# Latent attention's matmuls pinned to the order in which the program names them, and memory weights split one piece ahead

## Chip, cores and metric

The kernel runs on one core of a Trainium2 chip. The metric is the device time of one execution in microseconds (us). A core has five engines that run side by side, each with an instruction queue of its own: TensorE (PE: matmuls and transposes; its weight loads are listed as PEld), VectorE (DVE), ScalarE (ACT), GpSimd (POOL) and SyncE (SP, which issues DMAs). They wait for each other through semaphores.

## What is computed

One decoder layer on 1024 tokens of width 1024, in float32. Two head groups read one input projection: gated linear attention, and latent attention (8 heads, keys of 96, values of 64). Their outputs are joined and projected; then come cross-attention to 256 memory tokens and a gated feed-forward with a short convolution. The part that the change touches, with the memory keys and values:

```python
q = to_heads(rms_norm(c_q, mla_q_a_norm[l]) @ mla_w_uq[l], MLA_HEADS)
kv = to_heads(rms_norm(c_kv, mla_kv_a_norm[l]) @ mla_w_ukv[l], MLA_HEADS)
k_nope, v = kv[..., :MLA_NOPE], kv[..., MLA_NOPE:]
...
q = rms_norm(q, mla_q_norm[l])
k = rms_norm(k, mla_k_norm[l])
...
o_mla = from_heads(causal_block_attention(q, k, v))   # blocks of 128 queries
...
mn = rms_norm(mem, norm_mem[l])
xkv = (mn @ xa_w_kv[l]).reshape(b, mem.shape[1], 2, XA_HEADS, XA_HEAD_DIM)
xk = rms_norm(xkv[:, :, 0], xa_k_norm[l])
xv = xkv[:, :, 1]
```

## The kernel before

Products with weights, and the scores, use **rounded** operands: a float32 array is split into a high and a low part (`split`: one pass on ScalarE, then one on VectorE), and `mm3` sums three matmuls. Transposes and the value products of latent attention use **exact** float32 operands.

The latent attention runs as a loop over slots j. Slot j belongs to one of 64 heads: two groups of four heads, and for each group eight query blocks of 128 tokens (a unit u), so a unit takes four slots. For each head these steps are needed:

- `att_s` (S): scores of one or two blocks of keys, with the mask added by one further matmul; VectorE takes the maximum and ScalarE the exponential, into `p`. It stands two slots ahead of the head that it is for.
- `att_t` (PTp): transposes of `p`, four at most to a PSUM bank. There is one bank; a pass of ScalarE or VectorE moves it to `pT`.
- `att_o` (mo): value products of two heads at a time. Each writes 64 columns of the array, and the two heads alternate between its halves.
- `prep_c`, `prep_kv`, `prep_q`, `prep_kt`, `prep_qt`: what a later unit needs; `kTp` and `qTp` are the transposes of its keys and queries, which `split` turns into KTh, KTl and QT. `att_r` (rr) transposes the reciprocal row sums once in a unit.

`mem_kv` is a generator. It projects the memory tokens to keys and values (`mo_kv`, 16 pieces of a weight of 256 rows by 256 columns), normalises the keys (`mks`) and transposes them (`mkt`). `filler` takes steps of it at the end of each slot. While it still has steps, `pr_` uses one PSUM bank for kv, q, kTp, qTp and rr. The split weights `mwh` and `mwl` have one buffer each.

What the engines run is not the written order: a scheduler lays the instructions of each engine out ahead of time, by priority (the written order) and by when it reckons them ready. `tc.keep_in_program_order(i)` ties an instruction behind the one that was written just before it on its engine. `o_gla` (otp) transposes the other group's output in the last eight slots.

Of the kernel before, what the change touches and what calls it, by code (L numbers as in the profile page):

```python
# [10 lines left out]
F32 = mybir.dt.float32  # L11
# [4 lines left out]
ALU = mybir.AluOpType  # L16
# [17 lines left out]
def build(tc, a, out):  # L34
# [25 lines left out]
    def k16(shape, dt, name):  # L60
        return big.tile(shape, dt, name=name, tag="k16", bufs=8)

    mm = nc.tensor.matmul

    def act(o, i, f, **kw):
        nc.scalar.activation(out=o, in_=i, func=f, **kw)  # L66

    def tt(o, x, y, op, eng=None):
        (eng or nc.vector).tensor_tensor(out=o, in0=x, in1=y, op=op)  # L69
# [7 lines left out]
    def split(hi, lo, src, gain=None):  # L77
        if gain is None:
            act(hi, src, AF.Copy)
            tt(lo, src, f32(hi), ALU.subtract)  # L80
        else:
            act(hi, src, AF.Copy, scale=gain)
            stt(lo, src, gain, f32(hi), ALU.mult, ALU.subtract)
# [55 lines left out]
    def col(r):  # L139
        return cols[:, r:r + 1]  # L140
# [9 lines left out]
    def small(shape, name, bufs=3):  # L150
        return smp.tile(shape, F32, name=name, tag=name, bufs=bufs)
# [4 lines left out]
    def rsqrt(dst, ssq, n, inv, post=None, nm="ra"):  # L156
        yy = small([P, 8], nm + "_y", 2)[:, 0:n]
        act(yy, ssq, AF.Ln, scale=inv, bias=epsc)
        act(yy, yy, AF.Exp, scale=-0.5)
        ms = small([P, 8], nm + "_m", 2)[:, 0:n]  # L160
        nc.vector.tensor_scalar(out=ms, in0=ssq, scalar1=inv, scalar2=EPS, op0=ALU.mult, op1=ALU.add)
        tq = small([P, 8], nm + "_t", 2)[:, 0:n]
        tt(tq, yy, yy, ALU.mult)
        stt(tq, tq, -0.5, ms, ALU.mult, ALU.mult)
        stt(yy if post else dst, tq, 1.5, yy, ALU.add, ALU.mult)
        if post is not None:
            nc.vector.tensor_scalar(out=dst, in0=yy, scalar1=post, scalar2=None, op0=ALU.mult)
# [415 lines left out]
    def pr_(shape, name):  # L583
        prn[0] += 1
        pl = prn[1] if prn[1] is not None else (prc, pjc[2])[prn[0] % 2]
        return sub(pl, shape, name)
# [91 lines left out]
    def prep_kt(u):  # L678
        G = grps[u.gi]
        tok = slice(u.t * P, (u.t + 1) * P)  # L680
        kp = pr_([MQK, 4, P], "kTp")
        for h in range(4):
            nc.tensor.transpose(kp[:, h], u.kn[:, h], ident)
        split(G[1][:, :, tok], G[2][:, :, tok], kp, cols[0:MQK, R_MK:R_MK + 1])

    def prep_qt(u):
        qp = pr_([MQK, 4, P], "qTp")
        for h in range(4):
            nc.tensor.transpose(qp[:, h], u.qn[:, h], ident)
        qt = qtc.tile([P, 2, 4, P], F32R, name="QT", tag="qt", bufs=3)  # L690
        u.QTh, u.QTl = qt[0:MQK, 0], qt[0:MQK, 1]
        split(u.QTh, u.QTl, qp, cols[0:MQK, R_MQ:R_MQ + 1])
# [30 lines left out]
    def att_t(x, b):  # L723
        k0, k1 = 4 * b, min(x.u.t + 1, 4 * b + 4)
        tp = pjc[0].tile([P, 4, P], F32, name="PTp", tag="pj", bufs=1)
        for k in range(k0, k1):
            nc.tensor.transpose(tp[:, k - k0], x.p[:, k * P:(k + 1) * P], ident)  # L727
        x.pT[b] = m.tile([P, 4, P], F32, name="pT", tag="pT", bufs=4)
        evac[0] += 1
        if evac[0] % 5 == 0:  # L730
            nc.vector.tensor_copy(out=x.pT[b][:, 0:k1 - k0], in_=tp[:, 0:k1 - k0])
        else:
            act(x.pT[b][:, 0:k1 - k0], tp[:, 0:k1 - k0], AF.Copy)

    def att_r(u):

        ri = m.tile([P, 4, MV], F32, name="ri", tag="ri", bufs=2)
        r4 = small([P, 4], "xri", 2)
        nc.vector.reciprocal(out=r4, in_=u.rs)
        nc.gpsimd.tensor_copy(out=ri, in_=r4.unsqueeze(2).broadcast_to([P, 4, MV]))  # L740
        rp = pr_([P, 2, P], "rr")
        for i in range(2):
            nc.tensor.transpose(rp[:, i], ri[:, 2 * i:2 * i + 2].rearrange("p h v -> p (h v)"), ident)
        u.r = m.tile([P, 2, P], F32, name="rT", tag="ri", bufs=2)
        act(u.r, rp, AF.Copy)

# [33 lines left out]
    def mem_t(i):  # L780
        if i == 0:
            MN.append(k16([P, 2, KD, MEM], F32R, "mn"))
        bs = slice((i // 2) * P, (i // 2 + 1) * P)
        tp = pr_([P, 4, P], "mtp")
        k0 = 4 * (i % 2)
        for k in range(4):
            nc.tensor.transpose(tp[:, k], MB[i // 2][:, (k0 + k) * P:(k0 + k + 1) * P], ident)
        split(MN[0][:, 0, k0:k0 + 4, bs], MN[0][:, 1, k0:k0 + 4, bs], tp)

    def mem_kv():  # L790
        mn = MN[0]
        for n in range(4):
            o = pr_([P, 2, 256], "mo_kv")
            for hk in range(4):
                raw = mk.tile([P, 2, 256], F32, name="mraw", tag="raw", bufs=2)
                nc.sync.dma_start(out=raw, in_=a["xa_w_kv"][hk * 256:(hk + 1) * 256, n * 256:(n + 1) * 256]
                                  .rearrange("(k p) n -> p k n", p=P))
                hi = mk.tile([P, 2, 256], F32R, name="mwh", tag="wh", bufs=1)
                lo = mk.tile([P, 2, 256], F32R, name="mwl", tag="wl", bufs=1)
                for j in range(2):  # L800
                    split(hi[:, j], lo[:, j], raw[:, j], col(R_NE + 2 * hk + j))
                yield
                for b in range(2):
                    bs = slice(b * P, (b + 1) * P)
                    for i in range(2):
                        lh, ll = mn[:, 0, 2 * hk + i, bs], mn[:, 1, 2 * hk + i, bs]
                        mm(o[:, b], lhsT=ll, rhs=hi[:, i], start=hk == 0 and b == 0 and i == 0, stop=False)
                        mm(o[:, b], lhsT=lh, rhs=lo[:, i], start=False, stop=False)
                        mm(o[:, b], lhsT=lh, rhs=hi[:, i], start=False, stop=hk == 3 and b == 1 and i == 1)
                yield  # L810
            if n >= 2:
                act(xv[:, :, (n - 2) * 256:(n - 1) * 256], o, AF.Copy)
                continue
            ks = mk.tile([P, 4, P], F32, name="mks", tag="raw", bufs=2)
            kq = mk.tile([P, 4, P], F32, name="mkq", tag="wl", bufs=1)
            ss = small([P, 4], "xss", 2)
            act(ks, o.rearrange("p b (h d) -> p (b h) d", h=2), AF.Copy)
            act(kq, ks, AF.Square)
            nc.vector.tensor_reduce(out=ss, in_=kq, axis=AX.X, op=ALU.add)
            r = small([P, 4], "xr", 2)  # L820
            rsqrt(r, ss, 4, 1.0 / XD)
            tt(ks, ks, r.unsqueeze(2).broadcast_to([P, 4, P]), ALU.mult)
            yield
            tp = pr_([P, 2, 2, P], "mkt")
            for b in range(2):
                for h in range(2):
                    nc.tensor.transpose(tp[:, h, b], ks[:, 2 * b + h], ident)
            split(xk[:, 0, 2 * n:2 * n + 2], xk[:, 1, 2 * n:2 * n + 2], tp.rearrange("p h b i -> p h (b i)"), col(R_XK))

    fill = [mem_kv()]  # L830

# [46 lines left out]
    def o_gla(t):  # L878
        if not oh:
            o_pair(0)  # L880
        tok = slice(t * P, (t + 1) * P)
        tp = pr_([P, 4, P], "otp")
        for k in range(4):
            nc.tensor.transpose(tp[:, k], og[:, t, k * P:(k + 1) * P], ident)
        split(oh[0][:, :, tok], ol[0][:, :, tok], tp)

    def wo_pc(i, n):
# [13 lines left out]
    for j in range(-2, NS + 1):  # L901
        if j == JT:
            filler(1000)
            mkp.__exit__(None, None, None)
            mpp.__exit__(None, None, None)
            pw = pool("pw", "right"); pwc = pw.__enter__()
            with pri(-1000):
                W = [wo_pc(i, 0) for i in range(3)]
        if NS - NB <= j < NS:
            o_gla(j - NS + NB)  # L910
        A = hs_[j] if 0 <= j < NS else None
        B = hs_[j - 1] if j >= 1 else None
        C = hs_[j + 2] if j + 2 < NS else None
        if A:
            att_t(A, 0)
        if B and B.h % 2:
            att_o(hs_[j - 2], B, B.nh - 1)
        if C:
            att_s(C, 0)
        prep_slot(j)  # L920
        if A and A.h == 3:
            att_r(A.u)
        if A and A.nh == 2:
            att_t(A, 1)
            if A.h % 2:
                att_o(B, A, 0)
        if C and C.nh == 2:
            att_s(C, 1)
        if j >= 0:
            filler(2)  # L930
    mps.__exit__(None, None, None)
    prs.__exit__(None, None, None)
    for p_ in pjp[::-1]:
# [679 lines left out]
```

## Time and profile before

| | us |
|---|---|
| median of 3 runs (1373.0 to 1375.1) | 1374.26 |
| the profiled execution | 1373.4 |
| its span, first to last instruction | 1371.7 |
| TensorE busy, whole span | 1332.3 |
| VectorE busy, whole span | 929.2 |
| ScalarE busy, whole span | 648.1 |

TensorE is busy for 97% of the span. The slots of latent attention lie between 257 and 486 us. Busy time is the time in which some instruction of an engine is recorded as running; ends of matmuls are modelled, so where two matmuls stand behind each other it is the distance of their starts that tells what one costs.

### The profile page before, as it was taken

The page shows a single profiled execution, that of the slowest core. Times are in us where ns is not written, and L with a number is a line of the kernel's source. Part 1 is how long each engine was busy: PE and PEld are TensorE (multiplying, and loading weights), DVE is VectorE, ACT ScalarE, POOL GpSimd, SP SyncE. Part 2 cuts the span into 40 slices and gives each one's busy share as a digit, 9 for nine tenths or more (in the row PEclk, how much of TensorE's full clock was granted, in tenths as well). Part 3 has the DMA queues.
Part 4 walks back from the last instruction along what each step waited for, and adds up shares of the span by engine and source line. Part 5 has one row for each costly group of instructions (what it writes and reads, how often), then busy time and mean ns, then how long its engine had stood idle before and what let it go on. Part 6 is the DMA issues. An engine that isn't in the chain of part 4 may idle for free.

```text
span 1371.7 us, 19161 instructions
## 1 busy us (share of the span) xinstructions
PE 1332.3 (97%) x7240; PEld 1111.0 (81%) x7240; DVE 929.2 (68%) x1712; ACT 648.1 (47%) x1316; POOL 204.1 (15%) x318
## 2 busy tenths in 40 slices
PE   8999999999999999999997989999999999999998
PEld 8977789878777787888875767888888888888887
DVE  6545785786687635377778887677766777678562
ACT  6424447776776713275544434344333335334440
POOL 0210001322232000000021433322333220000000
PEclk9999999999999999999998999999999999999999
DMA  7121010111002213110121332223332226963331
GB/s 216 39 63 31 1 47 20 40 54 43 9 1 77 72 68 106 48 37 39 65 92 62 116 115 77 96 90 115 116 115 104 97 85 229 330 223 134 120 130 62
DMA packets 80621, 122.93 MB, mean 90 GB/s; under 512 B 7305, under 2 KB 48400, under 8 KB 80528
## 3 DMA queue, kind: packets, MB, share of 16 engines
q1 hardware_dynamic: 80354, 121.64, 26.4%
q8 instruction: 57, 0.93, 0.3%
q14 instruction: 36, 0.29, 0.1%
q10 hardware_dynamic: 174, 0.06, 0.0%
HBM read 93.11 MB, written 28.57 MB: 89 GB/s over the span
## 4 chain that ended last, share of the span: by engine, by line
PE 85%; DVE 7%; issue 3%; ACT 3%; DMA 1%; POOL 1%; SPq 0%; DVEq 0%; ACTq 0%; POOLq 0%
PE pj L88 6%; PE pj L89 6%; PE pj L90 6%; PE P L1220 6%; PE P L1222 6%; PE P L1221 6%; PE dn L1558 5%; PE dn L1557 5%; PE dn L1556 5%; PE mo L756 3%; PE PTp L727 2%; PE A L1221 2%; PE A L1222 2%; PE A L1220 2%; PE S L88 2%
## 5 line engine op out<-in xcount | busy, mean ns | idle before, releaser
L1220 PE MATMUL P<-obP,op 128*128 128x512 f32 x352 | 139.3, 396 | 8.2 <-DVE GU L69 8.1
L1222 PE MATMUL P<-obP,op 128*128 128x512 f32 x352 | 138.2, 393 | 0.0
L1221 PE MATMUL P<-obP,op 128*128 128x512 f32 x352 | 138.2, 393 | 0.0
L1556 PE MATMUL dn<-wk 128*128 128x512 f32 x308 | 119.9, 389 | 0.0
L1557 PE MATMUL dn<-wk 128*128 128x512 f32 x308 | 119.8, 389 | 0.0
L1558 PE MATMUL dn<-wk 128*128 128x512 f32 x308 | 119.8, 389 | 0.0
L66 ACT ACTIVATE op<-ss 128x512 fp32r<-128x512 f32 x88 | 55.0, 629 | 121.4 <-PE P L1222 78.1
L69 POOL TENSOR_TENSOR ss<-rw 128x512 f32<-128x512 f32 x42 | 55.2, 1336 | 279.1 <-DVE op L69 248.2
L69 DVE TENSOR_TENSOR op<-rw,op 128x512 fp32r<-128x512 f32 x58 | 63.2, 1089 | 40.0 <-ACT op L66 40.0
L1220 PEld LDWEIGHTS P<-obP,op 128*128 128x128 f32 x352 | 66.9, 190 | 25.2 <-DVE GU L69 11.3
L1222 PEld LDWEIGHTS P<-obP,op 128*128 128x128 f32 x352 | 66.8, 190 | 14.1
L1221 PEld LDWEIGHTS P<-obP,op 128*128 128x128 f32 x352 | 67.0, 190 | 13.8
L66 ACT ACTIVATE op<-rw 128x512 fp32r<-128x512 f32 x58 | 36.6, 631 | 79.5 <-PE P L1222 59.3
L1556 PEld LDWEIGHTS dn<-wk 128*128 128x128 f32 x308 | 57.8, 188 | 12.4 <-DVE hq L69 0.2
L1557 PEld LDWEIGHTS dn<-wk 128*128 128x128 f32 x308 | 57.8, 188 | 12.0
L1558 PEld LDWEIGHTS dn<-wk 128*128 128x128 f32 x308 | 57.8, 188 | 12.0
L66 ACT ACTIVATE wk<-wq 128x1024 fp32r<-128x1024 f32 x28 | 29.7, 1061 | 74.6 <-PE dn L1558 56.3
L69 DVE TENSOR_TENSOR op<-ss,op 128x512 fp32r<-128x512 f32 x88 | 63.2, 726 | 1.1 <-ACT op L66 0.4
L72 DVE SCALAR_TENSOR_TENSOR conv<-GU,cols,conv 128x1023 f32<-128x1023 f32 (+1 forms) x44 | 57.1, 1297 | 3.7 <-ACT conv L66 3.3
L717 DVE TENSOR_REDUCE mx<-S 128x1 f32<-128x128 f32 (+7 forms) x64 | 48.0, 752 | 15.5 <-PE S L715 15.2
L1221 PE MATMUL A<-fl,op 128*128 128x512 f32 x144 | 56.0, 389 | 0.0
L1222 PE MATMUL A<-fh,op 128*128 128x512 f32 x144 | 56.0, 389 | 0.0
(434 smaller groups left out, 3740.7 us busy)
## 6 DMA issues: line engine op xcount, KB each, us to landing
ga<-gP SPq DMA_DIRECT2D x35, 512.0 KB
rw<-in_ffn_w_gate SPq DMA_DIRECT2D x11, 1024.0 KB
rw<-in_ffn_w_up SPq DMA_DIRECT2D x11, 1024.0 KB
gP<-GU SPq DMA_DIRECT2D x44, 256.0 KB
gP<-conv SPq DMA_DIRECT2D x33, 256.0 KB
wq<-in_ffn_w_down SPq DMA_DIRECT2D x16, 512.0 KB
mraw<-in_xa_w_kv SPq DMA_DIRECT2D x16, 256.0 KB
hh<-in_x SPq DMA_DIRECT2D x2, 2048.0 KB
```

Source lines behind the costliest of these rows:

```text
L66: nc.scalar.activation(out=o, in_=i, func=f, **kw)
L69: (eng or nc.vector).tensor_tensor(out=o, in0=x, in1=y, op=op)
L72: nc.vector.scalar_tensor_tensor(out=o, in0=x, scalar=s, in1=y, op0=op0, op1=op1)
L88: mm(o, lhsT=ll, rhs=rh, start=i == 0, stop=False)
L89: mm(o, lhsT=lh, rhs=rl, start=False, stop=False)
L90: mm(o, lhsT=lh, rhs=rh, start=False, stop=last and i == n - 1)
L1220: mm(o, lhsT=wl, rhs=bh[:, k], start=start and k == 0, stop=False, **kw)
L1221: mm(o, lhsT=wh, rhs=bl[:, k], start=False, stop=False, **kw)
L1222: mm(o, lhsT=wh, rhs=bh[:, k], start=False, stop=k == 3, **kw)
L1556: mm(bk[t], lhsT=gl, rhs=wh, start=first and g == 0 and k == 0, stop=False, **kw)
L1557: mm(bk[t], lhsT=gh, rhs=wl, start=False, stop=False, **kw)
L1558: mm(bk[t], lhsT=gh, rhs=wh, start=False, stop=end, **kw)
```

## The change

Inside the slots (from j = 0 on) every matmul and transpose that goes through `mm` and `transpose` is pinned behind the one written before it. The slot is written in another order: the transposes for keys, queries and row sums come behind `att_t` and `att_o`, then the scores and the other preparations, then one step of `mem_kv` (from j = -1 on; it was two steps from j = 0 on), and only then the second score block, `att_t` and `att_o`. In short slots (`late`) the second score block comes last. In `mem_kv` the weight of piece x+1 is loaded and split right behind the matmuls of piece x, and the transposes `mkt` come one step behind the matmuls whose sums they need.

```diff
-    mm = nc.tensor.matmul
+    PIN = [False]
+    def pinned(i):
+        if PIN[0]:
+            tc.keep_in_program_order(i)
+        return i
+    def mm(*args, **kw):
+        return pinned(nc.tensor.matmul(*args, **kw))
+    def transpose(*args):
+        return pinned(nc.tensor.transpose(*args))
...
     def mem_kv():
-        for n in range(4):
-            o = pr_([P, 2, 256], "mo_kv")
-            for hk in range(4):
-                raw = mk.tile([P, 2, 256], F32, name="mraw", tag="raw", bufs=2)
...
-                yield
...
+        pieces = [(n, hk) for n in range(4) for hk in range(4)]
+        w = weights(0, 0)
+        yield
+        for x, (n, hk) in enumerate(pieces):
...
+            if hk == 3 and n < 2:
+                ks = mk.tile([P, 4, P], F32, name="mks", tag="raw", bufs=2)
...
+                act(ks, o.rearrange("p b (h d) -> p (b h) d", h=2), AF.Copy)
+                act(kq, ks, AF.Square)
+                nc.vector.tensor_reduce(out=ss, in_=kq, axis=AX.X, op=ALU.add)
...
+            if x + 1 < len(pieces):
+                w = weights(*pieces[x + 1])
+            yield
+            if hk == 3 and n < 2:
+                tp = pr_([P, 2, 2, P], "mkt")
...
+                        transpose(tp[:, h, b], ks[:, 2 * b + h], ident)
...
+        PIN[0] = j >= 0
         if A:
             att_t(A, 0)
         if B and B.h % 2:
             att_o(hs_[j - 2], B, B.nh - 1)
+        pr = order.get(j, [])
+        for f, u in pr:
+            if f in (prep_kt, prep_qt):
+                f(u)
+        if A and A.h == 3:
+            att_r(A.u)
         if C:
             att_s(C, 0)
-        prep_slot(j)
-        if A and A.h == 3:
-            att_r(A.u)
+        for f, u in pr:
+            if f not in (prep_kt, prep_qt):
+                f(u)
+        if j >= -1:
+            filler(1)
+        late = C and C.nh == 2 and A and A.nh == 2 and A.h % 2 == 0
+        if C and C.nh == 2 and not late:
+            att_s(C, 1)
         if A and A.nh == 2:
             att_t(A, 1)
             if A.h % 2:
                 att_o(B, A, 0)
-        if C and C.nh == 2:
+        if late:
             att_s(C, 1)
-        if j >= 0:
-            filler(2)
+        PIN[0] = False
```

The number of instructions is the same on every engine (TensorE has 6742 matmul instructions in both), and outside the slots their order is the same too. Three places on TensorE follow.

**Value products.** In the last heads TensorE's order before was this (S are score blocks, PTp transposes of probabilities, mo value products, otp the other group's transposes):

```order
L756 MATMUL mo<-pT,vv 64x128 x7
L88 MATMUL S<-KTh_4263,QT 128x512
L89 MATMUL S<-KTl_4264,QT 128x512
L90 MATMUL S<-KTh_4263,QT 128x512
L715 LDWEIGHTS identb
L715 MATMUL S<-maskb,identb 128x128
L884 MATMUL otp<-ident,og 128x128 x4
L756 MATMUL mo<-pT,vv 64x128
L727 MATMUL PTp<-ident,p 128x128 x4
L756 MATMUL mo<-pT,vv 64x128 x7
```

After the change the same place reads:

```order
L72 MATMUL S<-KTh_4263,QT 128x512
L72 LDWEIGHTS identb
L72 MATMUL S<-maskb,identb 128x128
L75 MATMUL PTp<-ident,p 128x128 x4
L72 MATMUL mo<-pT,vv 64x128 x8
L75 MATMUL otp<-ident,og 128x128 x4
L75 MATMUL PTp<-ident,p 128x128 x4
L72 MATMUL mo<-pT,vv 64x128 x8
L75 MATMUL otp<-ident,og 128x128 x4
```

A stretch of value products is no longer broken by PTp after one instruction; it stands whole behind the transposes. Over all slots the 288 value products stood in 76 unbroken stretches before, 54 of them of an odd number of instructions, and 48 followed by a rounded matmul. After the change there are 47, all of an even number, 2 of them followed by a rounded matmul.

**Memory keys.** Before, TensorE reached the first transposes of normalised memory keys (mkt) through these rows; between the last mo_kv and the first of them here stand 15 more rows (PTp, mo, qTp and two score blocks):

```order
L727 MATMUL PTp<-ident,p 128x128 x2
L88 MATMUL kv<-uA,cTl 128x512
L89 MATMUL kv<-uB,cTh 128x512
L90 MATMUL kv<-uA,cTh 128x512
L756 MATMUL mo<-pT,vv 64x128 x3
L88 MATMUL S<-KTh_2720,QT 128x384
L89 MATMUL S<-KTl_2721,QT 128x384
L90 MATMUL S<-KTh_2720,QT 128x384
L715 LDWEIGHTS identb
L715 MATMUL S<-maskb,identb 128x128
L756 MATMUL mo<-pT,vv 64x128
L827 MATMUL mkt<-ident,mks 128x128 x4
```

After the change, from the last matmul of the piece (mo_kv) to mkt, which now stands in slot 4 (the second time in slot 9):

```order
L72 MATMUL mo_kv<-mwh,mn 128x256
L75 MATMUL PTp<-ident,p 128x128 x2
L72 MATMUL mo<-pT,vv 64x128 x2
L75 MATMUL qTp<-ident,qn 96x128 x4
L72 MATMUL S<-KTh_2720,QT 128x256
L72 MATMUL S<-KTl_2721,QT 128x256
L72 MATMUL S<-KTh_2720,QT 128x256
L72 LDWEIGHTS identb
L72 MATMUL S<-maskb,identb 128x128
L75 MATMUL mkt<-ident,mks 128x128 x4
```

Fewer rows stand between the sum and the transposes that need its normalised copy, and all that is written behind mkt stays behind it.

**Key transposes and q.** Both use the one bank of `pr_`. Before, q came behind memory matmuls; the key transposes kTp stood 21 rows above the first row of q, with two score blocks between as well:

```order
L807 MATMUL mo_kv<-mwh,mn 128x256
L808 MATMUL mo_kv<-mwl,mn 128x256
L809 MATMUL mo_kv<-mwh,mn 128x256
L807 MATMUL mo_kv<-mwh,mn 128x256
L808 MATMUL mo_kv<-mwl,mn 128x256
L809 MATMUL mo_kv<-mwh,mn 128x256
L88 MATMUL q<-uA,cTl 128x384
L89 MATMUL q<-uB,cTh 128x384
L90 MATMUL q<-uA,cTh 128x384
```

After, in slots 2, 6, 10, 14 and 18, one score block stands between:

```order
L75 MATMUL kTp<-ident,kn 96x128 x4
L72 MATMUL S<-KTh_2720,QT 128x384
L72 MATMUL S<-KTl_2721,QT 128x384
L72 MATMUL S<-KTh_2720,QT 128x384
L72 LDWEIGHTS identb
L72 MATMUL S<-maskb,identb 128x128
L72 MATMUL q<-uA,cTl 128x384
L72 MATMUL q<-uB,cTh 128x384
```

The memory matmuls now come behind q.

## Rows read from the trace of the kernel before

**Rows 1.** Windows: span, busy us (instructions) per engine, granted clock, DMA share, GB/s.

```profile
core 0: us, PE busy (x) PEld busy (x) DVE busy (x) ACT busy (x) POOL busy (x), PEclk, DMA share, GB/s
257.00:300.00 43.00, 40.69 (x291) 33.88 (x291) 35.44 (x99) 32.32 (x90) 11.37 (x27) 1.00 0.15 48
257.00:486.00 229.00, 224.51 (x1725) 179.51 (x1725) 170.62 (x387) 167.94 (x409) 52.55 (x127) 1.00 0.15 50
```

**Rows 2.** Timeline of TensorE, 475 us: start, busy us, line, output<-inputs, sizes, count.

```profile
475.65 0.60 PE L884 MATMUL otp<-ident,og 128*128 128x128 f32 x4
476.18 0.43 PE L756 MATMUL mo<-pT,vv 128*64 128x128 f32 x2
476.55 0.66 PE L727 MATMUL PTp<-ident,p 128*128 128x128 f32 x4
477.13 1.09 PE L756 MATMUL mo<-pT,vv 128*64 128x128 f32 x14
478.15 0.33 PE L884 MATMUL otp<-ident,og 128*128 128x128 f32 x1
```

**Rows 3.** Timeline of TensorE at 361 us.

```profile
361.76 0.66 PE L727 MATMUL PTp<-ident,p 128*128 128x128 f32 x4
362.35 0.88 PE L756 MATMUL mo<-pT,vv 128*64 128x128 f32 x12
363.15 0.50 PE L89 MATMUL S<-KTl,QT 96*128 96x512 f32 x1
363.49 0.40 PE L90 MATMUL S<-KTh,QT 96*128 96x512 f32 x1
```

**Rows 4.** Timeline at 380 us; in brackets idle time and what ended it.

```profile
380.28 0.60 PE L683 MATMUL kTp<-ident,kn 128*96 128x128 f32 x4
...
380.64 0.43 PE L88 MATMUL q<-uA,cTl 128*128 128x384 f32 x1
...
380.90 0.34 PE L89 MATMUL q<-uB,cTh 128*128 128x384 f32 x1
...
381.08 0.34 PE L90 MATMUL q<-uA,cTh 128*128 128x384 f32 x1
...
381.64 0.75 DVE L72 SCALAR_TENSOR_TENSOR KTl<-kTp,cols,KTh 96x512 fp32r<-96x512 f32 x1 [0.44 <-ACT KTh L66]
```

**Rows 5.** Timeline from 272 to 280 us.

```profile
272.61 0.28 PE L809 MATMUL mo_kv<-mwh,mn 128*128 128x256 f32 x1
...
272.92 0.60 ACT L66 ACTIVATE mks<-mo_kv 128x512 f32<-128x512 f32 x1 [0.20 <-PE mo_kv L809]
...
273.61 0.62 ACT L66 ACTIVATE mkq<-mks 128x512 f32<-128x512 f32 x1
...
274.44 0.68 DVE L819 TENSOR_REDUCE xss<-mkq 128x4 f32<-128x512 f32 x1
...
275.49 0.29 ACT L66 ACTIVATE ra_y<-xss,epsc 128x4 f32<-128x4 f32 x1
...
278.85 0.68 DVE L69 TENSOR_TENSOR mks<-mks,xr 128x512 f32<-128x512 f32 x1
...
279.59 0.33 PE L827 MATMUL mkt<-ident,mks 128*128 128x128 f32 x1 [0.61 <-DVE mks L69]
```

**Rows 6.** Tile mwh: line, engine, count: ns shortest/median/longest, first and last start us.

```profile
L66 ACT ACTIVATE mwh<-mraw,cols x32: 492/496/512, 256.8 to 323.7; 128x256 fp32r<-128x256 f32 x32
L72 DVE SCALAR_TENSOR_TENSOR mwl<-mraw,cols,mwh x32: 471/478/634, 259.6 to 324.6; 128x256 fp32r<-128x256 f32 x32
```

**Rows 7.** Timeline at 820 us.

```profile
819.80 0.50 PE L1220 MATMUL P<-obP,op 128*128 128x512 f32 x1 [4.02 <-DVE GU L69]
```

**Rows 8.** Windows, a stretch behind it (columns as in rows 1).

```profile
820.40:823.80 3.40, 3.40 (x10) 2.63 (x9) 0.00 (x0) 0.00 (x0) 0.00 (x0) 0.50 0.21 73
```

**Rows 9.** Tile PTp, its evacuation.

```profile
L66 ACT ACTIVATE pT<-PTp x77: 257/577/602, 258.3 to 482.2; 128x512 f32<-128x512 f32 x39, 128x128 f32<-128x128 f32 x13, 128x384 f32<-128x384 f32 x13, 128x256 f32<-128x256 f32 x12
```

**Rows 10.** Waits of TensorE, 257 to 316 us: us in total, times, longest.

```profile
PE PTp L727 <- ACT pT L66: 0.7, 1, 0.7
```

More of the change, by code (lines that the diff above doesn't have):

```diff
@@ L682, in prep_kt @@
         for h in range(4):
-            nc.tensor.transpose(kp[:, h], u.kn[:, h], ident)
+            transpose(kp[:, h], u.kn[:, h], ident)
         split(G[1][:, :, tok], G[2][:, :, tok], kp, cols[0:MQK, R_MK:R_MK + 1])
@@ L688, in prep_qt @@
         for h in range(4):
-            nc.tensor.transpose(qp[:, h], u.qn[:, h], ident)
+            transpose(qp[:, h], u.qn[:, h], ident)
         qt = qtc.tile([P, 2, 4, P], F32R, name="QT", tag="qt", bufs=3)
@@ L726, in att_t @@
         for k in range(k0, k1):
-            nc.tensor.transpose(tp[:, k - k0], x.p[:, k * P:(k + 1) * P], ident)
+            transpose(tp[:, k - k0], x.p[:, k * P:(k + 1) * P], ident)
         x.pT[b] = m.tile([P, 4, P], F32, name="pT", tag="pT", bufs=4)
@@ L742, in att_r @@
         for i in range(2):
-            nc.tensor.transpose(rp[:, i], ri[:, 2 * i:2 * i + 2].rearrange("p h v -> p (h v)"), ident)
+            transpose(rp[:, i], ri[:, 2 * i:2 * i + 2].rearrange("p h v -> p (h v)"), ident)
         u.r = m.tile([P, 2, P], F32, name="rT", tag="ri", bufs=2)
@@ L786, in mem_t @@
         for k in range(4):
-            nc.tensor.transpose(tp[:, k], MB[i // 2][:, (k0 + k) * P:(k0 + k + 1) * P], ident)
+            transpose(tp[:, k], MB[i // 2][:, (k0 + k) * P:(k0 + k + 1) * P], ident)
         split(MN[0][:, 0, k0:k0 + 4, bs], MN[0][:, 1, k0:k0 + 4, bs], tp)
@@ L791, in mem_kv @@
         mn = MN[0]
-        for n in range(4):
-            o = pr_([P, 2, 256], "mo_kv")
-            for hk in range(4):
-                raw = mk.tile([P, 2, 256], F32, name="mraw", tag="raw", bufs=2)
[L796 to L801, printed above, removed]
-                yield
[L803 to L809, printed above, removed]
-                yield
[L811 to L828, printed above, removed]
@@ new lines, in weights @@
+        def weights(n, hk):
+            raw = mk.tile([P, 2, 256], F32, name="mraw", tag="raw", bufs=2)
+            nc.sync.dma_start(out=raw, in_=a["xa_w_kv"][hk * 256:(hk + 1) * 256, n * 256:(n + 1) * 256]
+                              .rearrange("(k p) n -> p k n", p=P))
+            hi = mk.tile([P, 2, 256], F32R, name="mwh", tag="wh", bufs=1)
+            lo = mk.tile([P, 2, 256], F32R, name="mwl", tag="wl", bufs=1)
+            for j in range(2):
+                split(hi[:, j], lo[:, j], raw[:, j], col(R_NE + 2 * hk + j))
+            return hi, lo
@@ new lines, in mem_kv @@
+        pieces = [(n, hk) for n in range(4) for hk in range(4)]
+        w = weights(0, 0)
+        yield
+        for x, (n, hk) in enumerate(pieces):
+            if hk == 0:
+                o = pr_([P, 2, 256], "mo_kv")
+            hi, lo = w
+            for b in range(2):
+                bs = slice(b * P, (b + 1) * P)
+                for i in range(2):
+                    lh, ll = mn[:, 0, 2 * hk + i, bs], mn[:, 1, 2 * hk + i, bs]
+                    mm(o[:, b], lhsT=ll, rhs=hi[:, i], start=hk == 0 and b == 0 and i == 0, stop=False)
+                    mm(o[:, b], lhsT=lh, rhs=lo[:, i], start=False, stop=False)
+                    mm(o[:, b], lhsT=lh, rhs=hi[:, i], start=False, stop=hk == 3 and b == 1 and i == 1)
+            if hk == 3 and n >= 2:
+                act(xv[:, :, (n - 2) * 256:(n - 1) * 256], o, AF.Copy)
+            if hk == 3 and n < 2:
+                ks = mk.tile([P, 4, P], F32, name="mks", tag="raw", bufs=2)
+                kq = mk.tile([P, 4, P], F32, name="mkq", tag="wl", bufs=1)
+                ss = small([P, 4], "xss", 2)
+                act(ks, o.rearrange("p b (h d) -> p (b h) d", h=2), AF.Copy)
+                act(kq, ks, AF.Square)
+                nc.vector.tensor_reduce(out=ss, in_=kq, axis=AX.X, op=ALU.add)
+                r = small([P, 4], "xr", 2)
+                rsqrt(r, ss, 4, 1.0 / XD)
+                tt(ks, ks, r.unsqueeze(2).broadcast_to([P, 4, P]), ALU.mult)
+            if x + 1 < len(pieces):
[3 more added lines that the diff above has]
+                tp = pr_([P, 2, 2, P], "mkt")
+                for b in range(2):
+                    for h in range(2):
+                        transpose(tp[:, h, b], ks[:, 2 * b + h], ident)
+                split(xk[:, 0, 2 * n:2 * n + 2], xk[:, 1, 2 * n:2 * n + 2], tp.rearrange("p h b i -> p h (b i)"), col(R_XK))
+                yield
@@ L883, in o_gla @@
         for k in range(4):
-            nc.tensor.transpose(tp[:, k], og[:, t, k * P:(k + 1) * P], ident)
+            transpose(tp[:, k], og[:, t, k * P:(k + 1) * P], ident)
         split(oh[0][:, :, tok], ol[0][:, :, tok], tp)
```

## The prediction

> **What bounds the kernel now.** I read the stretch of latent attention first in the windows. From 257 to 486 us TensorE is busy for 224.5 of 229.0 us, VectorE for 170.6, ScalarE for 167.9 [rows 1]: TensorE sets the time, so what is to be found is TensorE time that is not matmul work, and new waits of TensorE. In the first 43 us, where the memory steps run, VectorE has 35.4 us of work and ScalarE 32.3 under TensorE's 40.7 [rows 1]: there the other two are near as well. TensorE's waits are few there; the longest, of PTp for its bank, is 0.7 us [rows 10].
>
> Then I read TensorE's timeline for the distance from one start to the next, since ends are modelled. A value product costs 0.11 where it follows its kind: seven of them are busy for 1.09 us and a single one for 0.43, and (1.09 - 0.43) / 6 = 0.11 [rows 2] (each is recorded as two). I take 0.11 for a transposition too; the otp rows give (0.60 - 0.33) / 3 = 0.09 [rows 2], with a modelled end. A change from exact to rounded operands by itself costs nothing that I can see: from the four transpositions kTp to the second matmul of q it is 380.90 - 380.28 = 0.62 us, and 4 x 0.11 and one step of q of 0.18 are 0.62 [rows 4]. What costs is to go into and out of a stretch of value products.
>
> **The change, part by part.**
>
> *1. Stretches of value products.* The single product: from otp to PTp 476.55 - 475.65 = 0.90, less 4 x 0.11 and 0.11, is 0.35; the PTp behind it takes 0.66 where the same four took 0.60 as otp, 0.06 more [rows 2]. So 0.41. The seven behind it: 478.15 - 476.55 = 1.60, less those 0.06, 0.44 and 0.77, is 0.33, and 0.06 behind it again [rows 2]: 0.39. I take 0.40 for a stretch of an odd number. An even one, of six: 363.15 - 361.76 = 1.39, less 0.06, 0.44 and 0.66, is 0.23; the score behind it starts its next matmul after 0.34 [rows 3], where 512 columns at the rate of q (0.18 for 384 [rows 4]) take 0.24, so 0.10 to 0.11 more. With a rounded follower that is 0.34, with an exact one 0.29. The follower is then worth 0.05.
> Before: 54 x 0.40 + 22 x 0.29 + 48 x 0.05 = 30.4 us. After: 47 x 0.29 + 2 x 0.05 = 13.7. That is **-16.7 us**, all of it TensorE's time on the path. Its bounds: nothing, if the stretch is filled by other waits, and about 19 if 0.45 holds for odd ones.
>
> *2. Memory keys (mkt).* From the start of the last mo_kv to mkt the trace has 279.59 - 272.61 = 7.0 us [rows 5]. The work itself is 0.60 + 0.62 + 0.68 + 0.68 for the four wide passes [rows 5], about 1.2 for six small steps of the inverse root at up to 0.29 [rows 5], and some 0.4 of hops: 4.2 bare. The rest is queueing behind other work of ScalarE and VectorE. Before, TensorE had rows to run in that time and waited 0.61 [rows 5]. After, slot 4 puts before mkt only 2 PTp (0.22), 2 mo (0.22 + 0.29), 4 qTp (0.44) and one score block of 256 columns (0.42): 1.6 us, and slot 9 is much like it. Everything written behind mkt (the next PTp, the scores of two slots on, the next piece) is queued behind the wait. Of 4.2 and 7.0 I take 6.1, nearer the traced one, because the queues of ScalarE and VectorE still hold exponentials and splits then; 4.5 us of standing, twice: **+9.0** (5.2 to 10.8).
>
> *3. q behind kTp in one bank.* q can't start until KTl has read kTp: from the end of kTp's work (380.28 + 0.44) to the end of KTl (381.64 + 0.75) is 1.67 [rows 4], with a hop 1.73. Between them stands now one score block, in five slots of 256, 384, 512, 256 and 384 columns or so (0.42, 0.59, 0.75, 0.44, 0.53 at the rate above): 8.65 - 2.73 = **+5.9**. Below, if ScalarE takes KTh no later than the block lasts, it is 4; above, with a pass of the exponential ahead, 9.
>
> *4. Memory weights one piece ahead.* The buffers are single, so the split begins when the piece's matmuls end. ScalarE 0.50, VectorE 0.48 [rows 6] and hops make 1.3 to 1.4 to the first products that can go on. In most slots more work than that stands between; in the four slots without other preparations 0.75 to 1.3 does. **+1.4** (0 to 3). Where the filler was two steps in a slot it is one: neutral.
>
> *5. The clock.* After TensorE stood for 4.02 us [rows 7], the granted clock was 0.50, that is 1.2 GHz instead of 2.4, for 3.4 us [rows 8]: about half of these, 1.6, is lost. Two stops of 4.5 are longer than that: **+3.2** (0 to 3.2).
>
> *6. Other small stops.* One bank of PTp with an evacuation of 0.58 [rows 9]: between two uses it needs that and the hops on both sides, some 0.95 by estimate, where one late score block gives 0.75. In some 16 places 0.1 to 0.2 is left: 1.6. The first qTp waits for q, 0.9: **+2.5** (0 to 6).
>
> *7.* The two waits of before in this stretch that these take the place of, 0.7 [rows 10] and 0.61 [rows 5], go: **-1.3**.
>
> Sum: -16.7 + 9.0 + 5.9 + 1.4 + 3.2 + 2.5 - 1.3 = +4.0. The profiled execution took 1373.4, so 1377.4; the median of the runs shown is 0.9 above it: **1378 us**. Less than 0.2%, 2.75 us, is what a measurement of this kernel can hardly tell from no change.
>
> The Trainium skill speaks against my first price: "TensorEngine Tiling (Array Packing)", Key Properties, says that a change of the tiling mode drains TensorE. The 64-column products are such a mode beside the full array, so by the rule each stretch pays on entry and exit whatever its parity, and that would be 76 - 47 = 29 fewer drains; at 0.35 to 0.40, an estimate, about -11 instead of -16.7, and a total near +10. Rows 2 and 3 show a drain, and a dearer one for an odd number.
>
> **The rivals.**
>
> *R1, the other side: faster, because the stops are not paid in full.* In the first 18 slots VectorE and ScalarE are 82% and 75% busy [rows 1]. If they, and not TensorE, set the pace there, a stop of TensorE is made up by the queue behind it. The stops of parts 2, 3, 4 and 5 less 7 are 9.0 + 5.9 + 1.4 + 3.2 - 1.3 = 18.2; at half of that the total is 4.0 - 9.1 = -5.1, about **1369**. It decides below 78% of the price ((16.7 - 2.5) / 18.2). Against it: TensorE is busy for 95% of that stretch, more than either.
>
> *R2, about the same: the chain to mkt runs bare.* While TensorE stands, nothing new comes to ScalarE and VectorE, so 4.2 instead of 6.1 holds. Each stop is then 2.6, too short by rows 7 to be known to lower the clock: 4.0 - 3.8 - 3.2 = -3.0, about **1371**, on the edge between no change and faster. For it: the rows between 275.49 and 278.85 are mostly queueing [rows 5]. Against: TensorE's standing empties the queues only late.
>
> *R3, slower: late operands at every head.* The pinned order has PTp of a head first in its slot. Where `p` or `pT` comes later than the written order supposes, all that follows waits too, where before the scheduler had put other work ahead. At 0.15 in each of 64 slots that is 10 us: about **1388**. Against it: scores stand two slots ahead, and a slot is 229.0 / 64 = 3.6 us on the average [rows 1].
>
> **How the numbers follow.** My forecast has 0.42: with some 4 us around +4 it is slower in 0.28, the same in 0.12, faster in 0.02. R1 has 0.26 (faster 0.20, the same 0.06), R2 0.20 (half and half), R3 0.12 (slower). Faster 0.32, same 0.28, slower 0.40. The range reaches from 1365 (R1 with the lower bounds of parts 2 and 3) to 1388 (R3); about 0.15 lies outside. The likeliest case alone spans 1373 to 1383.
>
> **What would show it.** In the profile after: value products only in rows of even number, with start distances that give 0.29 a stretch; a wait of mkt for VectorE's mks of 4 to 5 us twice, and a granted clock of 0.5 behind each; a wait of q for KTl of 1 to 1.3 us in five slots. If the waits of mkt are under 3 us, R2 is right; if they are long and the stage's stretch from 257 to 300 us is hardly longer, R1; if waits of PTp for p or of mo for pT sum to over 6 us after 320 us, R3. The forecast is wrong if the switch around value products is worth less than 0.1 between odd and even, or if exact and rounded neighbours cost something after all: the gain is then another than 16.7.

## Result and profile after

The changed kernel takes 1400.04 us (median of 4 runs, 1396.91 to 1400.28), the kernel before 1374.53 beside it: a ratio of 1.0182, interval 1.0168 to 1.0197. The direction was the forecast one, the size was not: +25.5 us where +4 was forecast, outside the range. The profiled execution has a span of 1398.6 us, 26.9 more than before. TensorE's first PTp starts at 257.2 us (before at 257.4), and its last value product at 509.9 instead of 483.8: 26.3 of the 26.9 us lie in the slots of latent attention.

The windows of the changed kernel, beside [rows 1] (span, busy us of PE, PEld, DVE, ACT, POOL, granted clock, DMA share, GB/s):

```profile
257.00:300.00 43.00, 34.11 (x216) 29.51 (x215) 29.32 (x79) 26.39 (x73) 10.29 (x25) 0.84 0.12 38
257.00:486.00 229.00, 199.81 (x1505) 164.60 (x1505) 151.68 (x353) 147.78 (x361) 52.31 (x125) 0.93 0.10 31
```

All engines do less in the same time: TensorE 199.8 us for 224.5, VectorE 151.7 for 170.6, ScalarE 147.8 for 167.9. None of the three has become the bound: each has less to do in the stretch than before, and they wait for each other. The mean granted clock of the stretch is 0.93, where it was 1.00.

TensorE's waits from 257 to 512 us (engine, output, line, what it waited for: us in all, times, longest):

```profile
PE mkt L75 <- DVE mks L81: 7.6, 2, 4.2
PE q L72 <- DVE KTl L84: 7.0, 6, 1.5
PE PTp L75 <- ACT pT L78: 4.9, 6, 1.9
PE kv L72 <- ACT uA L78: 4.0, 1, 4.0
PE kv L72 <- DVE cTl L81: 2.3, 1, 2.3
PE PTp L75 <- ACT p L78: 1.4, 2, 0.7
PE PTp L75 <- DVE pT L743: 0.9, 2, 0.6
PE qTp L75 <- ACT qn L78: 0.8, 1, 0.8
PE mo_kv L72 <- DVE mwl L84: 0.7, 3, 0.4
PE PTp L75 <- DVE rm_t L84: 0.6, 1, 0.6
```

The first two rows are the stops that parts 2 and 3 forecast (9.0 and 5.9 us). The two of kv, 6.3 us, the forecast didn't have. The timeline around the first stop for mkt and that for uA:

```profile
279.14 0.23 PE L72 MATMUL S<-maskb,identb 128*128 128x128 bf16 x1
282.75 1.09 PE L75 MATMUL mkt<-ident,mks 128*128 128x128 f32 x4 [3.38 <-DVE mks L81]
...
360.09 0.33 PE L72 MATMUL S<-KTh,QT 96*128 96x384 f32 x1
...
361.71 0.33 SPq L611 DMA_DIRECT2D ukraw<-in_mla_w_ukv  x1
...
363.82 0.51 ACT L78 ACTIVATE uA<-ukraw,cols 128x256 fp32r<-128x256 f32 x1 [1.77 <-DMA ukraw<-in_mla_w_ukv]
...
364.38 0.80 PE L72 MATMUL kv<-uA,cTl 128*128 128x512 f32 x1 [3.97 <-ACT uA L78]
```

uA holds the second head group's weights, which are loaded in slot 20 through buffers shared with kn and qn. The transfer of the last piece is issued at 361.71, its split begins at 363.82, and kv, for which it is, stands in slot 21 with everything else pinned behind it. Before, the scheduler had put kv where the weight was there: the split of that piece began at 347.4 us and kv at 348.33, and in the slots TensorE never waited for uA.

The four transpositions of mkt are busy for 1.09 us where [rows 2] has 0.60 for four transpositions: they run at half clock. Windows on the five stretches at half clock in the slots:

```profile
260.65:267.48 6.83, 6.41 (x28) 6.16 (x29) 4.95 (x14) 3.60 (x11) 2.62 (x7) 0.50 0.12 38
281.13:287.96 6.83, 5.21 (x21) 4.48 (x22) 3.49 (x10) 2.62 (x8) 1.01 (x2) 0.50 0.23 77
305.02:311.85 6.83, 4.42 (x24) 3.70 (x25) 2.91 (x9) 1.48 (x4) 0.07 (x1) 0.50 0.26 77
363.05:369.88 6.83, 5.50 (x27) 4.10 (x28) 2.51 (x6) 2.35 (x5) 0.61 (x1) 0.50 0.03 10
424.49:431.32 6.83, 6.29 (x25) 4.90 (x26) 3.43 (x9) 2.08 (x5) 1.08 (x3) 0.50 0.00 0
```

They are 6.83 us each, twice the 3.4 of [rows 8], and five where the forecast had two. Each begins during a stop of TensorE: for qn, for mks twice, for uA, for cTl. In the columns of [rows 1], the granted clock is the third figure from the end.

The value products did get cheaper. In the changed kernel's timeline a stretch of eight (16 records):

```profile
484.88 0.50 PE L75 MATMUL PTp<-ident,p 128*128 128x128 f32 x3
485.31 1.09 PE L72 MATMUL mo<-pT,vv 128*64 128x128 f32 x16
486.33 0.66 PE L75 MATMUL otp<-ident,og 128*128 128x128 f32 x4
```

486.33 - 484.88 = 1.45, less 3 x 0.11 and 8 x 0.11, is 0.24, and the otp behind it takes 0.66 for 0.60: 0.29 to 0.30, the forecast price of an even stretch.

**An account by start distances.** For every matmul from the first PTp to the last value product I took the distance to the next start, less the work itself (0.11 for a transposition or a value product, 0.06 to 0.23 for a rounded one of 128 to 512 columns). What is left over is a wait where it exceeds 0.35 us, lost clock where the granted clock was 0.50, else it goes to the neighbourhood of value products or to the rest. In us:

| kernel | stretch | work | waits | half clock | value products | rest |
|---|---|---|---|---|---|---|
| before | 226.4 | 183.0 | 5.5 | 0 | 25.0 | 12.9 |
| changed | 252.7 | 183.0 | 34.2 | 13.1 | 11.5 | 10.9 |
| e1_q_later | 245.2 | 182.0 | 34.5 | 8.3 | 11.3 | 9.1 |
| e2_mkt_later | 247.1 | 183.0 | 33.8 | 9.2 | 11.1 | 9.9 |
| e3_second_group | 244.1 | 183.0 | 29.5 | 9.1 | 11.5 | 11.1 |
| e4_all | 234.8 | 182.0 | 30.0 | 1.6 | 10.7 | 10.4 |
| e5_unpinned | 224.2 | 183.0 | 6.4 | 0 | 23.2 | 11.6 |
| e8_pins_only | 257.5 | 183.0 | 39.1 | 8.7 | 11.8 | 14.9 |
| e9_pin_late | 223.3 | 183.0 | 7.5 | 0 | 20.6 | 12.2 |
| e10_stop_filled | 243.7 | 189.1 | 29.2 | 1.6 | 11.6 | 12.0 |
| e11_pin_early | 252.1 | 183.0 | 32.9 | 11.4 | 13.9 | 10.9 |

A time in this table is that of one profiled execution. So +26.3 us is +28.7 of waits, +13.1 of clock, -13.5 around the value products, -2.0 of rest.

### The profile page after: what moved, and what is told of

Same layout as the page of the kernel before. It is cut to its first block, busy times and chain, and to the rows that moved or that the text cites. A ratio compares the mean times of both kernels' runs of the same rounds, so it can differ in the third digit from the quotient of the medians.

```text
span 1398.6 us, 19156 instructions
## 1 busy us (share of the span) xinstructions
PE 1332.6 (95%) x7240; PEld 1115.9 (80%) x7240; DVE 932.0 (67%) x1712; ACT 650.5 (47%) x1316; POOL 205.3 (15%) x318
## 4 chain that ended last, share of the span: by engine, by line
PE 82%; DVE 9%; ACT 3%; issue 3%; DMA 1%; POOL 1%; SPq 0%; ACTq 0%; POOLq 0%; DVEq 0%
PE pj L72 18%; PE P L72 16%; PE dn L72 15%; PE A L72 7%; PE D L72 4%; PE S L72 3%; PE mo L72 2%; PE PTp L75 2%; PE xo L72 2%; PE mo_kv L72 1%; PE q L72 1%; DVE t L81 1%; PE XO L72 1%; PE att L72 1%; PE go L72 1%
## 5 line engine op out<-in xcount | busy, mean ns | idle before, releaser
L72 PE MATMUL P<-obP,op 128*128 128x512 f32 x1056 | 251.1, 393 | 9.1 <-DVE GU L81 9.1
L72 PE MATMUL dn<-wk 128*128 128x512 f32 x924 | 209.7, 389 | 0.0
L72 PE MATMUL A<-fh,op 128*128 128x512 f32 x288 | 94.6, 389 | 0.0
L72 PE MATMUL D<-obP,op 128*128 128x512 f32 x264 | 65.6, 395 | 7.6 <-ACT obP L78 7.6
L72 PE MATMUL S<-KTh,QT 96*128 96x384 f32 (+5 forms) x192 | 71.0, 384 | 0.0
L72 PEld LDWEIGHTS D<-obP,op 128*128 128x128 f32 x264 | 50.1, 190 | 18.7 <-ACT obP L78 8.0
L72 PEld LDWEIGHTS A<-fh,op 128*128 128x128 f32 x288 | 54.1, 188 | 11.3
L75 PE MATMUL PTp<-ident,p 128*128 128x128 f32 x288 | 50.7, 286 | 8.1 <-ACT pT L78 4.9
L78 ACT ACTIVATE p<-S,mx 128x128 f32<-128x128 f32 (+7 forms) x64 | 47.4, 741 | 22.1 <-DVE mx L729 21.1
L81 DVE TENSOR_TENSOR wk<-wq,wk 128x1024 fp32r<-128x1024 f32 x28 | 34.2, 1223 | 27.4 <-ACT wk L78 27.4
L72 PE MATMUL pj<-lo_wo,oh 128*128 128x512 f32 x128 | 50.0, 391 | 0.6 <-DVE lo_wo L81 0.5
```

The costliest lines, as they stand in the source:

```text
L72: return pinned(nc.tensor.matmul(*args, **kw))
L75: return pinned(nc.tensor.transpose(*args))
```

## Experiments

**The stops one by one.** Three kernels each move one late operand away from the matmul that needs it; the fourth does all three. A time that stands without an interval is that of one execution; four of the changed kernel lie between 1396.91 and 1400.28 us.

e1_q_later, the query projection a slot later:

```diff
-        for ds, f in ((0, prep_c), (1, prep_kv), (2, prep_q), (6, prep_kt), (8, prep_qt)):
+        for ds, f in ((0, prep_c), (1, prep_kv), (3 if a_ > 1 else 2, prep_q), (6, prep_kt), (8, prep_qt)):
```

> The changed kernel with the query projection of each unit (from the third on) one slot later, so that it no longer shares its slot and its PSUM bank with the key transposes. Theory A (each wait of TensorE behind a late operand costs its own length, and a stop long enough also a stretch at half clock): the six waits of q for KTl, about 8 us with what lies around them, go, and with them the stretch of 6.8 us at a granted clock of 0.50 behind the first of them, worth about 2.6: 1400 - 10 = about 1390 us, PE waits for KTl under 1 us in all. Rival B (ScalarE and VectorE set the pace, a removed wait comes back as another): the time stays within 3 us of 1400 and the waits of PTp for pT grow by what the waits for KTl lose.

Measured: 1394.99 us. The wait for KTl falls from 7.0 to 2.3 us, two stretches at half clock are gone (those at 260 and 424 us; one was expected to go), but q now waits for rT (1.9), which shares its bank in the new slot, and the waits for uA and mks grow (4.0 to 5.5 and 7.6 to 9.4). Waits in all: 34.5 for 34.2.

e2_mkt_later, two empty steps ahead of mkt:

```diff
             if hk == 3 and n < 2:
+                yield
+                yield
                 tp = pr_([P, 2, 2, P], "mkt")
```

> The changed kernel with the transposes of the memory keys two slots later (two empty steps of the memory generator ahead of each). Theory A: the two waits of mkt for mks (3.4 and 4.2 us idle, 7.9 with the hops) and the two stretches at half clock behind them (2.6 each) go: 1400 - 13 = about 1387 us, three stretches at 0.50 left instead of five. Rival B: under 4 us is gained, since VectorE and ScalarE had used the stops to catch up and other waits take their place.

Measured: 1393.46 us. No wait for mks is left, but kv waits for QT (2.5, new), mo_kv for rm_t (1.6, new), PTp for pT more than in the changed kernel (6.9 for 4.9). Waits in all 33.8. Five stretches at half clock are left where three were expected, but four of them last 3.41 us: 9.2 us are lost for 13.1.

e3_second_group, other buffers for the second group's weights, latent copies a slot earlier:

```diff
+            if gi and k == 0:
+                uq2 = qtc.tile([P, 2, 384], F32, name="uqraw", tag="qt", bufs=3)
...
+            raw = (mk.tile([P, 256], F32, name="ukraw", tag="graw", bufs=1) if k else mp.tile([P, 256], F32, name="ukraw", tag="kn", bufs=2)) if gi else qtc.tile([P, 256], F32, name="ukraw", tag="qt", bufs=3)
...
-        for ds, f in ((0, prep_c), (1, prep_kv), (2, prep_q), (6, prep_kt), (8, prep_qt)):
+        for ds, f in ((-1 if a_ > 3 else 0, prep_c), (1, prep_kv), (2, prep_q), (6, prep_kt), (8, prep_qt)):
```

> The changed kernel with the raw weights of the second head group in buffers that are free earlier, and the copy of the latent rows (cTh, cTl) of the later units one slot earlier. Theory A: the wait of kv for uA (4.0 us) and that of kv for cTl (2.3 us) go, each with its stretch at half clock (2.6): 1400 - 11.5 = about 1388 us, three stretches at 0.50 left. Rival B: the weights wait for the same chain of transfers, and PE waits for uA stay over 2 us: 1396 or more.

Measured: 1392.57 us. Both waits of kv are gone; PTp waits for pT 7.2 us in place of 4.9. Four stretches at half clock are left, for three expected.

e4_all joins the three edits.

> The three edits together: the query projection a slot later, the memory keys two slots later, the second group's weights and copies earlier; all pins stay. Theory A (the pinned order costs only by its stops, and saves about 13 us around the value products): the gains add, 10 + 13 + 11.5 = 34.5, so about 1366 us, faster than the kernel before by 0.6%, with no or one stretch at half clock. Rival B (the pace is set elsewhere): no more than 15 us come off, about 1385 us, slower than the kernel before.

Measured: 1385.53 us, 1.0093 times the kernel before (1.0076 to 1.0109). Rival B's figure of 1385 came out, theory A's 1366 did not; alone, the three edits had taken 5.0, 6.6 and 7.5 us off, between what A (10, 13, 11.5) and B (at most 3, 4 and 4) gave them. B's reason, that ScalarE and VectorE set the pace, is not shown: in the changed kernel they are busy for 147.8 and 151.7 of 229 us. The clock came back, 1.6 us lost instead of 13.1; the waits did not, 30.0 for 34.2. Its longest waits:

```profile
PE PTp L75 <- ACT pT L78: 5.4, 8, 1.4
PE kTp L75 <- DVE kn L81: 4.2, 3, 1.8
PE q L72 <- ACT rT L78: 3.2, 4, 1.1
PE PTp L75 <- DVE pT L745: 3.1, 4, 1.3
```

Two of these operands, kn and rT, TensorE had not waited for in the changed kernel. So the stops named in the trace were not the cause one by one: with the pins some 30 us of waiting is there, wherever it falls. That made a theory C, that the pins themselves make the stops, against a rival D, that the new written order makes them.

**Pins or order.** e5_unpinned is the changed kernel with the call of `keep_in_program_order` taken out; e8_pins_only is the kernel before, in its own written order and with its own memory steps, with the pins put in. The edit of e5:

```diff
-        if PIN[0]:
-            tc.keep_in_program_order(i)
```

> The changed kernel, same written order and memory steps, with no instruction pinned. Theory C (the pins make the stops: with them any operand that is late stops TensorE, some 30 us in each of the four kernels run so far): the waits of TensorE fall below 8 us, no stretch at half clock, the value products break up again (73 stretches, 48 odd, by their prices 27.7 us against 30.5 before): about 1371 us, within 4 us of the kernel before. Rival D (the new written order and the memory steps make the stops): 1385 or more, with waits of mkt for mks and of kv for uA over 2 us.

Measured: 1370.44 us, and no stretch at half clock in the slots. Its waits from 256 to 516 us begin so:

```profile
PE S L72 <- ACT p L78: 1.0, 2, 0.7
PE PTp L75 <- DVE pT L743: 1.0, 1, 1.0
PE S L72 <- DVE rq L672: 1.0, 1, 1.0
```

> The kernel before, its written order and its memory generator, with all matmuls and transpositions of the slots pinned. Value products stand in 47 even stretches (15.9 us by the prices). Theory C: waits of 30 us or more and half-clock stretches come with the pins, in places of their own: 1390 to 1405 us. Rival D (it is the new order, not the pins): about 1373 - 13 + 5 = 1365 us.

Measured: 1405.56 us, with

```profile
PE mkt L75 <- DVE mks L81: 8.1, 2, 4.2
PE q L72 <- DVE KTl L84: 7.4, 5, 1.6
PE kv L72 <- ACT uA L78: 3.9, 1, 3.9
PE mo_kv L72 <- DVE mwl L84: 3.8, 7, 1.6
```

The same operands stop TensorE under the other written order. This settles it for C: take the pins out, and 28 of 34 us of waits go; put them in alone, and 5.5 us become 39.1.

e7_mem_only, the kernel before with the new memory generator and one step in a slot:

> The kernel before with the memory generator of the change and one step in a slot instead of two; no pins, written order of the slots as before. Theory C: within 3 us of 1373, waits of TensorE below 10 us. Rival D: slower by 5 to 15 us, with waits of mkt for mks of 3 us or more.

Measured: 1375.17 us, waits 5.2 us by the account. The memory steps without pins add no waits; the one time is 1.9 us above the kernel before, its slots 1.4 us longer.

e6_mo_only was to make the value products unbroken and nothing else:

```diff
-                mm(u.o[r, i], lhsT=V[:, k, x.h * MV:(x.h + 1) * MV], rhs=x.pT[b][:, k - k0], start=k == 0, stop=k == u.t)
+                y = mm(u.o[r, i], lhsT=V[:, k, x.h * MV:(x.h + 1) * MV], rhs=x.pT[b][:, k - k0], start=k == 0, stop=k == u.t)
+                if k > k0 or x is x1:
+                    tc.keep_in_program_order(y)
```

> The kernel before with only the value products of one call pinned behind each other; all else is left to the scheduler. Value products then stand in 47 stretches, none odd, 3 with a rounded follower: by the prices of the prediction 13.8 us against 30.5. Theory C: the waits of TensorE stay below 10 us, so about 1373.4 - 13 = 1360 us (the measured share of that term was 13.5). Rival D agrees. A third view (the switch around value products was only idle time that other waits fill): no change, 1373.

Measured: 1373.05 us, ratio 0.9999 (0.9989 to 1.0009). It tests nothing of its aim: a pin holds an instruction behind another but keeps no third one out from between, and TensorE's order came out as before, 76 stretches. It shows how closely two kernels with one order agree.

**What the stops cost in clock.** e10_stop_filled leaves the stops for mks as they are and gives TensorE useless work in them:

```diff
                 tp = pr_([P, 2, 2, P], "mkt")
+                for _ in range(28):
+                    transpose(tp[:, 0, 0], ident, ident)
```

> The changed kernel with 28 useless transpositions (some 3.1 us of TensorE) ahead of mkt each time, into the bank that mkt then overwrites: the two stops for mks stay as long, but TensorE works in most of them. If the loss of clock comes from TensorE standing still, the two stretches of 6.8 us at 0.50 behind them go: three left instead of five, 1400 - 2 x 2.7 = about 1395 us. Rival (the clock falls for another reason, or the added work lengthens the stops): five stretches at 0.50 and 1400 to 1406 us.

Measured: 1396.31 us. Its timeline at the first stop, and windows behind both:

```profile
277.94 3.23 PE L75 MATMUL mkt<-ident 128*128 128x128 f32 x28
281.39 0.66 PE L75 MATMUL mkt<-ident,mks 128*128 128x128 f32 x4 [0.23 <-DVE mks L81]
```

```profile
281.40:288.00 6.60, 5.70 (x43) 4.58 (x43) 3.59 (x9) 3.75 (x9) 0.97 (x2) 1.00 0.24 79
304.30:311.00 6.70, 5.93 (x47) 5.12 (x48) 2.49 (x4) 3.94 (x8) 0.60 (x2) 1.00 0.25 78
```

With 6.1 us of work added, the slots take 9.0 us less than in the changed kernel: the clock behind both stops is 1.00, and mkt's four matmuls are busy for 0.66. Two more stretches, at 260 and 424 us, are missing too, with the same waits ahead of them (1.72 with 0.93, and 2.47 us by the account), so those were not sure to come, and the added work can be credited only with the two behind mks, some 5 of the 11.5 us of clock. The whole span is only 4.0 us shorter, because behind the slots, where the two kernels are the same, this execution took 4.9 us longer, with 23.4 us at half clock there for 17.0 and 1.4 us more of waits for GU.

**Where the pins do no harm.**

e11_pin_early and e9_pin_late split the pins by slot, and e12_unpinned_timed is e5_unpinned again:

```diff
-        PIN[0] = j >= 0
+        PIN[0] = 0 <= j < 44
```

> The changed kernel with pins only in slots 0 to 43. Theory C: nearly all of the loss is there (waits 32 of 34 us, all half-clock stretches), and the late slots run equally well without pins: about 1400 us, within 3. Rival (the pins of the late slots save what the value products gain there, 4.4 us against the kernel before): 1403 to 1405 us.

Measured: 1399.37 us, with waits of 32.9 us: the loss is in slots 0 to 43.

```diff
-        PIN[0] = j >= 0
+        PIN[0] = j >= 44
```

> The changed kernel with pins only from slot 44 on, where the operands come in time: value products in 67 stretches, 36 odd, by the prices of the prediction 24.5 us against 27.7 without pins. If the pins gain what the prices say where they meet no late operand: 1370.4 - 3 = about 1367 us. Rival (the written order alone has already brought this, as the slot lengths of the two kernels from slot 48 on are alike within 0.1 us): 1370 to 1371 us. Both are faster than the kernel before, by 0.45% or by 0.2%.

Measured: 1371.46 us, ratio 0.9982 (0.9974 to 0.9991), without a stretch at half clock in the slots. That is nearer the rival's 1370 to 1371 than the 1367 of the prices: value products cost 20.6 us for the 23.2 without pins, and 1.1 us of waits comes back.

> The changed kernel without pins once more, in five rounds: 1370 to 1371 us, faster than the kernel before by 0.2%, with an interval that leaves out no change if the single time of 1370.44 was no chance.

Measured: 1372.08 us, ratio 0.9984 (0.9975 to 0.9993). The single 1370.44 of e5 lies below all eleven executions here (1371.04 to 1372.64), but the interval leaves out no change, as expected. Both beat the kernel before by a little under 0.2%, and can't be told from each other.

## Why the prediction was wrong, by its steps

The sum of +4.0 became +26.3 by four differences: 9.9 in the clock, 11.2 in the waits, 3.2 in the value products, less 2.0 in the rest.

- **Step 1, the value products** (-16.7), held as a price on TensorE: -13.5 by the account, and an even stretch costs 0.29 (median over the changed kernel's stretches). In the kernel before, odd stretches cost 0.10 to 0.12 more than even ones with the same kind of follower (medians of start distances). What this price gains in the whole time, no run shows by itself: e6, made for it, left the order as it was, and in e9 2.6 us less around the value products went with 1.1 us more of waits. The Trainium skill's rule ("TensorEngine Tiling (Array Packing)", Key Properties: a change of the tiling mode drains TensorE) agrees in that the 47 stretches still cost that much; an estimate of 29 fewer drains at one price, -11, lies a little nearer to the account. The difference between odd and even stretches is not in that rule.
- **Step 2, mkt** (+9.0), was right in place and size: 3.4 and 4.2 us idle, between the 4.5 forecast and R2's 2.6 for the first, near 4.5 for the second.
- **Step 3, q behind kTp** (+5.9): six waits of 7.0 us, for the five forecast; the sixth stands in slot 0.
- **Step 4, memory weights** (+1.4): 0.7 us.
- **Step 5, the clock** (+3.2), was the right mechanism, mis-sized by 9.9 us: five stretches of 6.83 us, not two of 3.4, 13.1 us lost. By the mean of 2.6, the two behind mks took 5.2 of these, for the 3.2 forecast; the other 7.9 came behind stops for which the forecast had no loss of clock. I took the one stretch of [rows 8] as the price, and only stops longer than 4 us as its cause. The trace of the kernel before held a longer one: at its start TensorE stands for 4.06 us, and the clock is at 0.50 for 6.83.

```profile
9.54 1.97 PE L197 MATMUL tp<-ident,xb 128*128 128x128 f32 x8 [4.06 <-DMA xb<-in_x]
8.01:14.84 6.83, 5.30 (x25) 5.31 (x26) 4.53 (x13) 5.04 (x12) 0.19 (x1) 0.50 1.08 303
```

In e10 TensorE works through most of both stops for mks, and the clock stays at 1.00 behind them: it is its standing still that costs the clock there.

- **Step 6, other small stops** (+2.5, at most 6), is the step that failed. It listed two stops, of PTp for its bank (1.6) and of qTp (0.9). Measured were 14.9 us by the waits above: 5.8 of PTp for pT, that is for its bank, 0.8 of qTp, and 8.3 that it did not list (uA 4.0, cTl 2.3, p 1.4, rm_t 0.6). It should have gone through every operand that a pinned matmul reads, and asked when it is ready. Those of uA (4.0) and cTl (2.3) were to be found: the second group's weights come through buffers shared with qn, and qTp frees one of them only in the slot ahead of kv. Beyond those, e1 to e4 show that a list could not have given the sum: as one stop was removed, others grew. Where the scheduler before broke the written order, it put ready work ahead of late operands, and that was worth 28 us of waits.
- **The rivals.** R1, that stops are made up by the other engines, is refuted as to the time: VectorE and ScalarE had less work in the same time in 257 to 300 us, 29.3 and 26.4 us, and TensorE lost 6.6 of its 40.7. R2 was half right on the length of the stop (3.4 in slot 4) and wrong on the clock. R3, late operands at every head, came nearest, 1388, with a chance of 0.12, but not by its mechanism, and so by luck: its sign was over 6 us of waits of PTp for p or of mo for pT after 320 us, and there PTp waits for p 1.4 us and mo for pT not at all. The 5.8 us of PTp for pT are waits for its one bank. It also lacked the clock.

What stays open is why waits settle at 30 us in the pinned kernels e1 to e4. ScalarE's and VectorE's own queues were laid out by a scheduler with times of its own; how much an order made for these traces' times would save was not tried.

## What to carry to other kernels

Before pinning one engine's order, list for each pinned instruction its latest operand and the work that stands ahead of it on the pinned engine, and look for what the free order had put in between; a few late operands are enough to lose more than the tidier order gains. If a pinned order is wanted, pin only where the trace shows no late operands; there (e9) it did no harm, but no gain over the kernel without pins (e12) could be measured either. Count stops of TensorE twice, once for their length and once for the clock behind them. Removing the longest wait in a trace of a pinned queue buys less than its length: e4 removed 19 us of named waits (mks, KTl, uA, cTl) and kept 30 of 34.

## What was not expected of the hardware

- The 15 longest stops of TensorE in the slots of these kernels, from 3.5 to 5.7 us by the account, all went with a granted clock of 0.50, for 6.83 us in 14 of them and 3.41 in one (e10, for uA). Stops of 1.7 to 2.9 us did so in some executions and not in others: the 2.47 us ahead of kv for cTl went with 6.83 us in the changed kernel, with 3.41 in e2 and e11, with none in e10.
- A stretch at half clock cost less than half its length. In the changed kernel TensorE was busy for only 4.4 to 6.4 us of each 6.83, as the end of the stop and further waits fall into it; the loss was 2.6 us each by the account.
